# Moving the last block's channel LayerNorm into the first phase, and reordering the loads of the second phase, in a hybrid conformer/RWKV-7 block

## The chip, the core and the metric

The kernel runs on one core of a Trainium2 chip. The metric is the device time of one execution in microseconds (us). Engines are named as in the profile: PE multiplies matrices (PEld loads its weights), DVE is the vector engine, ACT the scalar engine, POOL is GpSimd, and SP issues the DMAs. Before the change the median of 3 runs is 2893.17 us (2893.12 to 2894.62).

## What is computed

One decoder block on x of 2048 tokens by 1024 channels. Cut to what matters here:

```python
h = _rmsnorm(x, norm_g) * (1.0 + scale) + shift
p = h @ w_in                                    # c_val, c_gate, c_og, ts, r_og, g_conv, g_rwkv
u = c_val * sigmoid(c_gate)
u = causal_depthwise_conv(u, conv_k, conv_b)    # width 31
u = _layernorm(u, ln_g, ln_b)                   # over the 1024 channels
u = silu(u) * silu(c_og)
y_conv = u @ w_conv_out
y_rwkv = _rwkv7_branch(...)                     # token shift, delta-rule state, group norm
m = sigmoid(g_conv) * y_conv + sigmoid(g_rwkv) * y_rwkv
x = x + gate * (m @ w_out)
return _rmsnorm(x, final_g)
```

## The kernel before

**Tiles.** The tokens are cut into four blocks (b = 0 to 3) of 512, and each matrix of 1024 channels by 512 tokens into eight tiles (j = 0 to 7) of 128 x 512 float32, 256 KB each. A product in nearly float32 precision is made of three passes: the weights and the data are split into a high and a low part (`w_hi`, `w_lo`, `h_hi`, `h_lo`), and hi*hi, hi*lo and lo*hi are summed in PSUM. A projection is 24 such matmuls (8 k-steps of 3).

**First phase** (lines 425 to 1487). For each block there are four groups g of the RWKV heads (`slot`, line 1388). A group projects the inputs of two head pairs (`k`, `r`, `vv`) and, between them, "fills": channel tiles of the convolution (`c`, two projections each) and gates (`1` to `4`). `FILL` and `LAST` (lines 46 and 47) give the order of the fills. Each conv tile is followed by 31 taps on DVE (`taps`, line 1170), whose result `yj` is stored to DRAM as `y_d[b][j]`. The chain of a group's delta rule runs between the projections. Side work (`sides`, line 1323) does the next block's RMSNorm, the channel LayerNorm of the block before (`lnorm_first`, line 1189, on POOL, in group 1 of blocks 1 to 3), and the splitting of the weights `ro` and `o` into hi and lo parts ahead of their use (`presplit`, line 305: 1, 0, 1, 2 weight tiles in the groups of blocks 1 and 2, and 4, 2, 2, 0 in those of block 3). `lnorm_first` reads the eight `y_d` tiles three times: for the mean, for the variance, and to write `u_d[b][j]`, the normalised and gated tile. It takes its tiles (`lny`, `lnc`, `lnth`) from a ring of seven buffers, `hx`. At the end of the phase `rows0` (line 1456) projects block 0's RWKV output with `w_rwkv_out` (`ro`, tiles `rth`) and its conv output with `w_conv_out` (`co`), and leaves the merged m in `mr`.

**What sets the order.** In the first phase the program writes its own order: a planner keeps a clock for each engine (`note`, line 85, with the rates of lines 48 to 53), the steps of every task are generators that say when they could go on, and `poll` (line 152) emits a step once the planner's PE clock has come that far. Each engine then executes what was emitted for it strictly in that order, and so does SP with its DMAs. In the second phase the framework's scheduler sets the order; it may move loads and small work ahead of where they are written, also before the end of the first phase.

**Second phase** (lines 1491 to 1680). For each block: `cproj` (not for block 0), then the out products `pout` (line 1618: four column blocks of 256, each 96 matmuls of 128 x 256, with weights `o` loaded as `w_hi`/`w_lo`), `addx` (x added to `pout` on DVE), `finish` (the final RMSNorm, eight DVE operations on `xt`, and stores), and `rproj` of the next block, whose result DVE takes out of PSUM as `mr<-rth,ps_main`. `lsplit` loads the next block's z and u tiles (`zt`) and splits them (`m_hi`, `m_lo`, `o_hi`, `o_lo`, `u_hi`, `u_lo`). Block 3's LayerNorm is not done in the first phase; `lnorm` (line 1566) does it here, on tiles of its own (`y0` to `y7`, `ys`, `qs`, `ct`), with POOL for the sums, and with two matmuls, `pmean` and `pvar`. It is written at b = 2, but the scheduler placed most of it beside block 0's out products.

Of the kernel before, what the change touches and what calls it, by code (L numbers as in the profile page):

```python
# [18 lines left out]
P = 128  # L19
D = 1024  # L20
# [23 lines left out]
WB = 6  # L44
KEPT = ("in",)
FILL = ("c", "1", "3", "4", "2", "c", "1", "3", "4", "2")
LAST = ("c", "1", "c", "3", "4", "2", "1", "3", "4", "2")
# [24 lines left out]
def hybrid_block(ctx: ExitStack, tc: tile.TileContext, x, vecs, convk, w2a2, final_g, ada, w_in, w_co, w_ro, w_o, crow, out,  # L72
# [150 lines left out]
    class Ring:  # L223
# [11 lines left out]
        def give(self, *ts):  # L235
            for t in ts:
                self.free.append(max(ready.get(key(t), 0.0), used.get(key(t), 0.0)))

# [950 lines left out]
    def lnorm_first(b):  # L1189

        def yload(j):
            yj = hx.take("lny")
            nc.sync.dma_start(yj, y_dram[b][j])
            return yj

        yield hx.room(3, 1)
        ys, nxt = yload(0), yload(1)
        for j in range(1, KT):
# [5 lines left out]
            nc.gpsimd.tensor_tensor(out=ys, in0=ys, in1=yj, op=ALU.add)  # L1204
# [8 lines left out]
        for j in range(KT):  # L1213
# [5 lines left out]
            nc.gpsimd.tensor_tensor(out=yj, in0=yj, in1=mean, op=ALU.subtract)  # L1219
            yield ok(yj)  # L1220
            nc.scalar.activation(yj, yj, AF.Square)
            if j == 0:
                qs = yj
            else:
                yield ok(yj)
                nc.gpsimd.tensor_tensor(out=qs, in0=qs, in1=yj, op=ALU.add)
                hx.give(yj)
# [6 lines left out]
        for _ in rsteps(rl, qs, rt):  # L1234
            yield idle("DVE", 0.3)
        hx.give(qs, rt)
        for j in range(KT):
            yield hx.room(3, 1)
            yj, ct, th = yload(j), hx.take("lnc"), hx.take("lnth")
            nc.sync.dma_start(ct, co_dram[b][j])  # L1240
            yield ok(yj, rl)
            nc.gpsimd.tensor_tensor(out=yj, in0=yj, in1=mean, op=ALU.subtract)
            yield idle("POOL", 0.3)
            nc.gpsimd.tensor_tensor(out=yj, in0=yj, in1=rl, op=ALU.mult)
# [7 lines left out]
            nc.gpsimd.tensor_tensor(out=yj, in0=yj, in1=ct, op=ALU.mult)  # L1252
# [4 lines left out]
        hx.give(mean, rl)  # L1257
# [65 lines left out]
    def sides(b, g):  # L1323
# [6 lines left out]
        if b and g == 1:  # L1330
            yield from lnorm_first(b - 1)
        if b:
            for _ in range((4, 2, 2, 0)[g] if b + 1 == NB else (1, 0, 1, 2)[g]):
                n_ = later.pop(0)
                for half in range(2):
                    yield from presplit(*n_, half)

    reached, normed = [-1], [0]

    def side_work():  # L1340
        for n in range(4 * NB):
            yield when(lambda: reached[0] >= n)
            yield from sides(n // 4, n % 4)

# [13 lines left out]
    def order(b, g):  # L1358
        todo, cj, gj = list(FILL if b + 1 < NB or g < 3 else LAST), [2 * g, 2 * g + 1], {w: [2 * g, 2 * g + 1] for w in "1234"}

        def fill(n):
            for _ in range(n):
                w = todo.pop(0)
                yield w, (cj if w == "c" else gj[w]).pop(0)
# [60 lines left out]
    with tc.manual_schedule():  # L1425
# [21 lines left out]
        side.append(Task(side_work(), 3))  # L1447
# [8 lines left out]
        def rows0(a, name, gate_, nxt):  # L1456
            new, hfs = ([], []), []
            for n in range(KT):
# [25 lines left out]
              enumerate(("M", "ta", "E2", "k", "r", "vv", "y", "sh"))]  # L1484
        h = rows0(h, "ro", gr_dram[0], u_dram[0])
# [21 lines left out]
    def ldt(name, src):  # L1507
        t_ = ob.tile([P, TB], F32, name=name, tag="ld", bufs=6)
# [39 lines left out]
    b2 = ctx.enter_context(tc.tile_pool(name="b2", bufs=2, reuse_waits="tile"))  # L1548
    hl = ctx.enter_context(tc.tile_pool(name="hl", bufs=1, reuse_waits="tile"))
    pa = ctx.enter_context(tc.tile_pool(name="pa2", bufs=1, space=PSUM, reuse_waits="tile"))  # L1550
# [7 lines left out]
    nc.sync.dma_start(fg, final_g.unsqueeze(0).broadcast_to([P, D]))  # L1558
    def t2(name):
        return b2.tile([P, TB], F32, name=name, tag="t2", bufs=3)  # L1560

# [3 lines left out]

    def lnorm(b):

        y = []
        ys = b2.tile([P, TB], F32, name="ys", tag="ys", bufs=1)
        for j in range(KT):  # L1570
            yj = b2.tile([P, TB], F32, name=f"y{j}", tag=f"y{j}", bufs=1)
            nc.sync.dma_start(yj, y_dram[b][j])
            y.append(yj)
            if j:
# [140 lines left out]
```

## Time and profile before

| what | us |
|---|---|
| median of 3 runs | 2893.17 |
| the profiled execution's own time | 2892.82 |
| its span, from the first to the last instruction | 2890.7 |
| PE busy (94% of the span) | 2725.4 |
| DVE busy (71%) | 2058.8 |
| POOL busy (44%) | 1257.7 |
| ACT busy (38%) | 1090.7 |

The span is 2.1 us shorter than the execution's time. In the profile nearly every row of phase 1 and 2 has line L129, the helper that records each instruction, so instructions are told apart by tile names (out<-in), not by lines. A row of a table by windows gives the busy time of each engine within a stretch, the number of its instructions in brackets, then the granted PE clock (1.00 is full), the share of the 16 DMA engines that was busy, and GB/s. A row of a timeline gives the start and the duration, the engine, the instruction, and in brackets how long the engine had been idle before it and what ended that.

### The profile page before, as it was taken

The page shows a single profiled execution, that of the slowest core. Times are in us where ns is not written, and L with a number is a line of the kernel's source. Part 1 is how long each engine was busy: PE and PEld are TensorE (multiplying, and loading weights), DVE is VectorE, ACT ScalarE, POOL GpSimd, SP SyncE. Part 2 cuts the span into 40 slices and gives each one's busy share as a digit, 9 for nine tenths or more (in the row PEclk, how much of TensorE's full clock was granted, in tenths as well). Part 3 has the DMA queues.
Part 4 walks back from the last instruction along what each step waited for, and adds up shares of the span by engine and source line. Part 5 has one row for each costly group of instructions (what it writes and reads, how often), then busy time and mean ns, then how long its engine had stood idle before and what let it go on. Part 6 is the DMA issues. An engine that isn't in the chain of part 4 may idle for free.

```text
span 2890.7 us, 52304 instructions
## 1 busy us (share of the span) xinstructions
PE 2725.4 (94%) x19472; PEld 2201.6 (76%) x19472; DVE 2058.8 (71%) x3575; ACT 1090.7 (38%) x2180; POOL 1257.7 (44%) x1772
## 2 busy tenths in 40 slices
PE   6999999889999999999999999999999998899998
PEld 5777777667777777787777777777777777698988
DVE  6877787869677878885868787669787666543343
ACT  5545344434243434443434443333434233221211
POOL 0564746533528355444656462648373633100000
PEclk9999999989999999999999999999999999999999
DMA  8786767666757566776756686866666848676665
GB/s 329 255 295 219 281 221 263 237 227 234 231 187 257 183 218 237 250 258 221 252 181 233 205 294 201 273 211 215 205 246 213 294 158 314 234 240 229 215 226 175
DMA packets 361742, 680.47 MB, mean 235 GB/s; under 512 B 134160, under 2 KB 152912, under 8 KB 361488
## 3 DMA queue, kind: packets, MB, share of 16 engines
q1 hardware_dynamic: 361488, 677.13, 69.0%
q8 instruction: 154, 2.52, 0.4%
q14 instruction: 100, 0.82, 0.1%
HBM read 494.34 MB, written 181.54 MB: 234 GB/s over the span
## 4 chain that ended last, share of the span: by engine, by line
PE 32%; DVE 9%; POOL 7%; DMA 5%; issue 3%; ACT 1%; SPq 1%; DVEq 0%; POOLq 0%; ACTq 0%
PE ps_main L129 21%; PE pout L129 5%; DVE acc L129 3%; PE xo L129 2%; PE aux L129 2%; POOL TT L129 2%; POOL itmp L129 1%; PE late L129 1%; SPq L129 1%; DVE S L129 1%; DMA w_lo<-kl_in 1%; POOL oc L129 1%; DVE gst L129 1%; DVE rs_t L129 1%; POOL lny L129 1%
## 5 line engine op out<-in xcount | busy, mean ns | idle before, releaser
L129 PE MATMUL ps_main<-h_hi,w_hi 128*128 128x512 f32 x2432 | 1016.7, 418 | 17.4 <-DVE lora L129 4.6
L129 PE MATMUL ps_main<-h_hi,w_lo 128*128 128x512 f32 x2432 | 967.7, 398 | 20.3 <-POOL w_lo L129 13.6
L129 PE MATMUL ps_main<-h_lo,w_hi 128*128 128x512 f32 x2432 | 963.8, 396 | 2.0 <-DVE h_lo L129 2.0
L129 DVE SCALAR_TENSOR_TENSOR acc<-u,ck,acc 128x512 f32<-128x512 f32 x928 | 697.5, 752 | 25.3
L129 PEld LDWEIGHTS ps_main<-h_hi,w_lo 128*128 128x128 f32 x2432 | 463.4, 191 | 130.7 <-POOL w_lo L129 16.8
L129 PEld LDWEIGHTS ps_main<-h_hi,w_hi 128*128 128x128 f32 x2432 | 464.0, 191 | 128.9 <-issue 10.0
L129 PEld LDWEIGHTS ps_main<-h_lo,w_hi 128*128 128x128 f32 x2432 | 464.9, 191 | 99.8 <-issue 7.8
L129 POOL TENSOR_TENSOR w_lo<-w_st,w_hi 128x1024 fp32r<-128x1024 f32 (+1 forms) x83 | 165.2, 1990 | 302.9 <-ACT w_hi L129 248.7
L129 POOL TENSOR_TENSOR TT<-TT,itmp 128x126 f32<-128x126 f32 (+22 forms) x496 | 207.3, 418 | 38.9
L129 ACT ACTIVATE th<-ps_main 128x512 f32<-128x512 f32 x160 | 95.6, 598 | 333.9 <-PE ps_main L129 281.7
L129 ACT CAST w_hi<-w_st 128x1024 fp32r<-128x1024 f32 (+1 forms) x135 | 127.2, 943 | 243.2 <-DMA w_st<-w_co_t 137.3
L129 POOL TENSOR_TENSOR itmp<-La,TT 128x126 f32<-128x126 f32 (+22 forms) x496 | 200.8, 405 | 37.1 <-issue 6.4
L129 DVE SCALAR_TENSOR_TENSOR S<-xo,pe,Se 64x64 f32<-64x64 f32 x512 | 145.0, 283 | 90.1 <-PE xo L129 65.3
L129 ACT COPY uv<-xo 64x256 f32<-64x256 f32 (+1 forms) x192 | 81.0, 438 | 238.3 <-PE xo L129 164.7
L129 POOL TENSOR_TENSOR lny<-lny 128x512 f32<-128x512 f32 x90 | 119.9, 1340 | 108.9 <-DMA lny<-y_d 87.0
L129 DVE TENSOR_TENSOR w_lo<-w_st,w_hi 128x1024 fp32r<-128x1024 f32 x52 | 72.4, 1392 | 68.3 <-PE ps_main L129 46.5
L129 ACT ACTIVATE Se<-S,pe 128x128 f32<-128x128 f32 x256 | 88.7, 396 | 83.2 <-DVE S L129 82.7
L129 DVE TENSOR_TENSOR As<-aux,maskA 128x512 f32<-128x512 f32 x128 | 82.3, 685 | 52.5 <-PE aux L129 52.5
L129 POOL TENSOR_TENSOR wlo<-wf,wl 64x128 fp32r<-64x128 f32 x64 | 31.2, 488 | 149.6 <-ACT wl L129 147.0
L129 ACT ACTIVATE t<-ps_main,mu 128x512 f32<-128x512 f32 x96 | 65.9, 687 | 77.6 <-PE ps_main L129 68.0
L129 DVE TENSOR_TENSOR xt<-pout,xt 128x256 f32<-128x256 f32 x64 | 24.4, 419 | 99.3 <-PE pout L129 93.2
L129 PEld LDWEIGHTS xo<-S,KR 128*128 128x128 f32 x512 | 76.8, 189 | 23.9 <-DVE S L129 5.3
(298 smaller groups left out, 5029.0 us busy)
## 6 DMA issues: line engine op xcount, KB each, us to landing
w_hi<-kh_in SPq DMA_DIRECT2D x219, 512.0 KB
w_lo<-kl_in SPq DMA_DIRECT2D x219, 512.0 KB
w_st<-w_in_t SPq DMA_DIRECT2D x73, 512.0 KB
kh_in<-w_hi SPq DMA_DIRECT2D x71, 512.0 KB
kl_in<-w_lo SPq DMA_DIRECT2D x71, 512.0 KB
lny<-y_d SPq DMA_DIRECT2D x72, 256.0 KB
w_hi<-kh_ro SPq DMA_DIRECT2D x32, 512.0 KB
w_lo<-kl_ro SPq DMA_DIRECT2D x32, 512.0 KB
```

The costliest lines, as they stand in the source:

```text
L129: r = f(*a, **k)
```

## The change

Five parts.

1. `lnorm` is deleted. `lnorm_first(3, more)` does block 3's LayerNorm as a task of its own (`last_norm`) in the first phase, once all 32 conv tiles are done, on DVE instead of POOL. Its buffers (`more`) are the tiles of the taps' tags `u` and `yj`, three of the `hx` ring lent after block 3's group 0 (`lend`), and three more after the last head pair. For its loads the planner adds `SLACK` to the time at which it takes them to have landed.
2. Block 3's eight conv tiles stand in groups 0, 1 and 2 (three, three and two) instead of two in each group, the LayerNorm of block 2 in its group 0 instead of 1, and all 16 presplits in blocks 1 and 2 (1, 1, 3, 3 in the groups of each).
3. In every `lnorm_first`, the second pass stores y minus mean back to `y_d`, the square goes to a tile of its own (`lnq`), and the third pass no longer subtracts the mean.
4. In the second phase x is loaded ahead of z, `final_g` only after them, and the next block's u is written behind the out products.
5. The ring `ld`, through which z and u tiles come in, has 8 buffers instead of 6.

```diff
+LDB = 8
+SLACK = 2.0
-LAST = ("c", "1", "c", "3", "4", "2", "1", "3", "4", "2")
+LAST = ("c0 10 20 c1 21 11 22 c2 23", "c3 12 24 c4 25 13 26 c5 27", "c6 14 30 c7 31 15 32 33 34 35",
...
-    def lnorm_first(b):
+    def lnorm_first(b, hx):
...
             nc.sync.dma_start(yj, y_dram[b][j])
+            if b + 1 == NB:
+                ready[key(yj)] += SLACK
...
+        eng = nc.vector if b + 1 == NB else nc.gpsimd
...
-            nc.gpsimd.tensor_tensor(out=yj, in0=yj, in1=mean, op=ALU.subtract)
-            yield ok(yj)
-            nc.scalar.activation(yj, yj, AF.Square)
+            eng.tensor_tensor(out=yj, in0=yj, in1=mean, op=ALU.subtract)
+            yield both(ok(yj), hx.room(1))
+            yq = hx.take("lnq")
+            nc.scalar.activation(yq, yj, AF.Square)
+            nc.sync.dma_start(y_dram[b][j], yj)
...
             yield ok(yj, rl)
-            nc.gpsimd.tensor_tensor(out=yj, in0=yj, in1=mean, op=ALU.subtract)
-            yield idle("POOL", 0.3)
-            nc.gpsimd.tensor_tensor(out=yj, in0=yj, in1=rl, op=ALU.mult)
+            eng.tensor_tensor(out=yj, in0=yj, in1=rl, op=ALU.mult)
...
-        if b and g == 1:
-            yield from lnorm_first(b - 1)
+        if b and g == (0 if b + 1 == NB else 1):
+            yield from lnorm_first(b - 1, hx)
+            if b + 1 == NB:
+                yield from lend(3)
         if b:
-            for _ in range((4, 2, 2, 0)[g] if b + 1 == NB else (1, 0, 1, 2)[g]):
+            for _ in range(0 if b + 1 == NB else (1, 1, 3, 3)[g]):
...
+    more = Slots([slot_of(e2, "u", 3)] * 3 + [slot_of(e2, "yj", 1)])
...
+    def last_norm():
+        yield when(lambda: len(convs) == KT * NB and convs[-1].done)
+        yield from lnorm_first(NB - 1, more)
...
-        t_ = ob.tile([P, TB], F32, name=name, tag="ld", bufs=6)
+        t_ = ob.tile([P, TB], F32, name=name, tag="ld", bufs=LDB)
...
-        if b + 1 < NB:
-            ohl = lsplit(z_dram[b + 1], okt(b + 1))
-            uhl = lsplit(u_dram[b + 1], utiles()) if b + 2 < NB else lnorm(b + 1)
         xts = []
...
+        if b + 1 < NB:
+            ohl = lsplit(z_dram[b + 1], okt(b + 1))
+        if b == 0:
+            nc.sync.dma_start(fg, final_g.unsqueeze(0).broadcast_to([P, D]))
...
         if b + 1 < NB:
+            uhl = lsplit(u_dram[b + 1], utiles())
             rall = tail_rs(0, NTT)
```

**SP, start of the out products of block 0.** The loads that stand ahead of the x tiles (`xt_...`) before; `y_...` and `ct` are the old LayerNorm's tiles, `zt` the z tiles of block 1.

```order
L129 DMA zt<-z_d_4_79 128x512
L129 DMA zt<-z_d_5_80 128x512
L129 DMA rth<-gr_d_0_267 128x512
L129 DMA rth<-gr_d_1_268 128x512
L129 DMA y_27755<-y_d_6_193 128x512
L129 DMA y_27758<-y_d_7_194 128x512
L129 DMA ct<-co_d_0_219 128x512
L129 DMA ct<-co_d_1_220 128x512
L129 DMA xt_25415<-x_in 128x512
```

The same place now, from the last store of the new LayerNorm (`u_d_7`) to the first x tile; `rth<-gc_d_7` is the gate of the last `co` projection, `kh_o`/`kl_o` the weights of the first column blocks.

```order
L132 DMA w_hi<-kh_o_0_13678 128x1024
L132 DMA z_d_7_98<-oc 128x512
L132 DMA w_lo<-kl_o_0_13679 128x1024
L132 DMA u_d_7_322<-lny 128x512
L132 DMA rth<-gc_d_7_234 128x512
L132 DMA w_hi<-kh_o_1_17041 128x1024
L132 DMA w_lo<-kl_o_1_17042 128x1024
L132 DMA w_hi<-kh_o_0_17406 128x1024
L132 DMA zt<-z_d_0_75 128x512
L132 DMA zt<-z_d_1_76 128x512
L132 DMA zt<-z_d_2_77 128x512
L132 DMA xt_25534<-x_in 128x512
```

The x loads stand behind three z tiles instead of six z tiles, eight y tiles and two ct tiles. The gate `rth<-gc_d_7` now stands behind two stores. A little further on SP, now, behind the eight x tiles and the z tiles:

```order
L132 DMA zt<-z_d_7_82 128x512
L132 DMA fg<-final_g 128x1024
L132 DMA w_lo<-kl_o_0_17407 128x1024
L132 DMA zt<-u_d_0_299 128x512
L132 DMA zt<-u_d_1_300 128x512
L132 DMA w_hi<-kh_o_1_17880 128x1024
```

`w_lo<-kl_o_0_17407` is the low half of the weights of the second column block; before, both halves of them stood ahead of all z and x tiles.

**DVE, end of block 0's out products**, before: the last four `finish` operations and what follows (`y_...<-th` and `y_...,ct` are the old LayerNorm's, `mr<-rth,ps_main` empties PSUM for PE).

```order
L129 SCALAR_TENSOR_TENSOR xt_25427<-xt_25427,rs_25907,fg 128x512
L129 SCALAR_TENSOR_TENSOR xt_25429<-xt_25429,rs_25907,fg 128x512
L129 SCALAR_TENSOR_TENSOR y_27746<-th,y_27746 128x512
L129 SCALAR_TENSOR_TENSOR y_27749<-th,y_27749 128x512
L129 SCALAR_TENSOR_TENSOR y_27752<-th,y_27752 128x512
L129 TENSOR_TENSOR y_27743<-y_27743,ct 128x512
L129 SCALAR_TENSOR_TENSOR mr_25935<-rth,ps_main 128x512
```

And now:

```order
L132 SCALAR_TENSOR_TENSOR xt_25542<-xt_25542,rs_26109,fg 128x512
L132 SCALAR_TENSOR_TENSOR xt_25544<-xt_25544,rs_26109,fg 128x512
L132 SCALAR_TENSOR_TENSOR xt_25546<-xt_25546,rs_26109,fg 128x512
L132 SCALAR_TENSOR_TENSOR xt_25548<-xt_25548,rs_26109,fg 128x512
L132 SCALAR_TENSOR_TENSOR mr_26137<-rth,ps_main 128x512
```

No LayerNorm operation stands any more between the end of the products and `mr`.

**DVE, during the `co` projections of `rows0`**, before (`S` and `uv` are the chain of the last group, `rth` and `mr` empty PSUM):

```order
L129 SCALAR_TENSOR_TENSOR rth<-rth,ps_main 128x512
L129 SCALAR_TENSOR_TENSOR mr_0_24204<-rth,mr_0_24204 128x512
L129 SCALAR_TENSOR_TENSOR S_405<-xo,pe,Se 64x64 x4
L129 TENSOR_TENSOR uv<-xo,uv 64x256
L129 SCALAR_TENSOR_TENSOR S_405<-xo,pe,Se 64x64 x4
```

And now, where the new LayerNorm's third pass (`lny`) stands between them:

```order
L132 SCALAR_TENSOR_TENSOR S_405<-xo,pe,Se 64x64 x4
L132 SCALAR_TENSOR_TENSOR lny<-lnth,lny 128x512
L132 TENSOR_TENSOR uv<-xo,uv 64x256
L132 TENSOR_TENSOR lny<-lny,lnc 128x512
L132 SCALAR_TENSOR_TENSOR S_405<-xo,pe,Se 64x64 x4
L132 TENSOR_TENSOR lny<-lny,lnr 128x512
L132 TENSOR_REDUCE gst<-uv 128x16
L132 TENSOR_SCALAR gst<-gst 128x16
L132 SCALAR_TENSOR_TENSOR rth<-rth,ps_main 128x512
```

`lny<-lny,lnr` is the first operation on a freshly loaded tile; the emptying of PSUM stands behind it.

112 lines of the change are left out of this document (57 added, 55 removed).

## The prediction

> **What bounds the kernel now.** The page says that PE is busy for 94% of the span, so the first question is where the other 6% lie. I read the table by windows, cut at the stages: the three later blocks of the first phase, `rows0`, and then block 0's out products with the two `rproj` projections that follow them, beside the same stretch of blocks 1 and 2.
>
> ```profile
> 600.50:1158.20 557.70, 537.91 (x4093) 427.50 (x4093) 436.34 (x789) 219.46 (x456) 257.60 (x398) 0.99 0.66 221
> 1158.20:1719.10 560.90, 541.31 (x4094) 430.11 (x4094) 435.92 (x773) 229.96 (x474) 292.85 (x445) 0.98 0.69 233
> 1719.10:2279.20 560.10, 537.69 (x4061) 425.41 (x4060) 418.21 (x709) 210.71 (x421) 308.97 (x450) 0.99 0.69 231
> 2279.20:2397.30 118.10, 111.67 (x858) 87.68 (x857) 73.67 (x122) 32.19 (x60) 42.51 (x47) 0.97 0.64 206
> 2398.20:2486.70 88.50, 62.58 (x434) 57.40 (x434) 69.03 (x99) 39.66 (x86) 36.58 (x24) 0.90 0.86 313
> 2566.00:2624.60 58.60, 57.25 (x432) 54.78 (x432) 25.91 (x57) 17.61 (x49) 0.00 (x0) 1.00 0.74 254
> 2701.40:2757.60 56.20, 56.15 (x433) 53.91 (x431) 20.88 (x49) 12.97 (x41) 0.00 (x0) 1.00 0.60 208
> ```
>
> The columns after the length are PE, PEld, DVE, ACT and POOL. In the first phase PE is idle for some 20 us of each block. Block 0's out products are the odd stage: for the same PE work (434 matmuls beside 432 and 433) they take 88.5 us, the others 58.6 and 56.2. That is some 30 us, the largest loss in one place, and the old LayerNorm runs in it. The waits of PE by releaser, in this stretch, say what it waits for:
>
> ```profile
> PE ps_main L129 <- DVE mr L129: 12.8, 1, 12.8
> PE pmean L129 <- POOL ys L129: 6.3, 1, 6.3
> PE pout L129 <- DVE o_lo L129: 2.6, 3, 1.1
> PE pout L129 <- DVE xt L129: 2.5, 1, 2.5
> PE pout L129 <- DMA w_lo<-kl_o: 1.8, 1, 1.8
> PE pout L129 <- DVE rth L129: 0.5, 1, 0.5
> ```
>
> The two long ones, 12.8 and 6.3 us, are the LayerNorm's: `pmean` stands in PE's queue and waits for POOL's sum, and `mr` stands on DVE behind the old LayerNorm's `y` operations and the `finish` operations. Together with the rest they make 26.5 us.
>
> **Part by part: the first out products.** With `pmean` and the y operations gone, what is late next? Three things.
>
> First, the low halves `o_lo` at the start, which wait for the last `co` projection and its gate. Their 2.6 + 0.5 us I keep. They could shrink, since the same operation takes
>
> ```profile
> L129 DVE TENSOR_TENSOR o_lo<-mr,o_hi 128x512 fp32r<-128x512 f32 x8 | 9.3, 1226 | 0.0
> L129 DVE TENSOR_TENSOR o_lo<-mr,o_hi 128x512 fp32r<-128x512 f32 x8 | 5.5, 692 | 4.9 <-ACT o_hi L129 4.9
> ```
>
> 1226 ns in this stretch, where POOL works, and 692 ns in block 2's, where POOL rests. They could also grow: `rth<-gc_d_7` now stands behind two stores that wait for POOL and DVE, and `o_lo` stands behind its consumer. I take 3.1 us, between 0.6 and 6.
>
> Second, the loads. The weights of the second column block need buffers that the last `co` projection holds, so they cannot be fetched before about 2397.
>
> ```profile
> 2400.00:2420.00 20.00, 11.95 (x92) 10.87 (x91) 12.47 (x14) 5.45 (x11) 13.08 (x9) 0.94 1.03 386
> 2420.00:2440.00 20.00, 15.75 (x106) 14.58 (x105) 16.66 (x21) 11.13 (x29) 10.65 (x7) 0.84 0.95 355
> 2400.26 0.32 SPq L129 DMA_DIRECT2D w_hi<-kh_o  x1
> 2413.57 5.02 SPq L129 DMA_DIRECT2D xt<-x_in  x8
> ```
>
> The DMA engines are full there (1.03 and 0.95 of them, 386 and 355 GB/s). From `w_hi` of the second column block to its `w_lo`, SP now issues 0.5 MB, three z, eight x and five z tiles of 0.25 MB, `fg` of 0.5 MB and `w_lo` of 0.5 MB: 5.5 MB, which at 386 GB/s take 15 us, so `w_lo` lands at about 2414. The first column block's 96 matmuls take a quarter of a column's
>
> ```profile
> 2566.00:2624.60 58.60, 46.05 (x384) 45.84 (x383) 6.04 (x16) 1.00 0.74 254
> ```
>
> 46.05 us (this row counts `pout` alone), 11.5 us, and end with the 3.1 us of waits at 2398.2 + 14.6 = 2412.8. That is a wait of about 2 us, and I add 1.5 for the later column blocks, whose weights stand behind u and z tiles: 3.5 us, between 0 and 8. The whole stage bears this out: 88.5 us at 313 GB/s moved 27.7 MB; without eight y tiles and the four ct tiles that came before its end (3.1 MB) 24.6 MB are left, 64 us at 386 and 69 at 355 GB/s.
>
> Third, the end. After the products DVE does 12 operations on four columns, eight `finish` operations and `mr`, as in block 1, whose 58.6 us hold such a wait already. I leave it there.
>
> Then the clock. After a short wait the matmuls come slower for a while:
>
> ```profile
> 2265.61 0.47 PE L129 MATMUL ps_main<-h_hi,w_hi 128*128 128x512 f32 x1 [1.74 <-DMA w_hi<-kh_in]
> 2266.96 0.51 PE L129 MATMUL ps_main<-h_hi,w_lo 128*128 128x512 f32 x1 [0.65 <-DMA w_lo<-kl_in]
> 2267.66 0.63 PE L129 MATMUL ps_main<-h_lo,w_hi 128*128 128x512 f32 x1
> ```
>
> 0.63 us instead of the usual 0.39, after two waits of 1.74 and 0.65 us; the stage as a whole was granted 0.90. I price one such stretch at 1.6 us (0 to 4). The Trainium skill, "TensorE: Matmul & The Clock Gate", section "What's actually happening", has the clock halved only after an idle window of about 3.4 us. By that rule waits of 2 and 1.5 us would cost nothing more than themselves, and the sum would be 1.6 us lower. The rows show the slow matmuls after less, and the measurement decides.
>
> So the stage takes 58.6 + 3.1 + 3.5 + 1.6 = 66.8 us instead of 88.5: **21.7 us gained**, between 11.9 (76.6 us) and 29.3 (59.2 us).
>
> **The projections behind it.**
>
> ```profile
> 2486.74 79.24 PE ps_main L129 x336
> 2624.60 76.82 PE ps_main L129 x336
> ```
>
> The chain of waits gives 79.24 us for those after block 0 and 76.82 after block 1; with no wait of 12.8 us ahead of them they should run alike: **2.4 us gained** (0 to 2.8).
>
> **What the first phase gets.** PE gets the mean and variance matmuls, 592 ns each: 1.2 us. DVE gets 57 operations (15 on sums and means, 7 on squares, 24 in the third pass, 11 for the square root): at 692 ns 39 us, and if all met POOL, at 1226 ns 70 us. The time for them:
>
> ```profile
> L129 PE MATMUL late<-lny,ones x12: 592/592/697, 874.4 to 1981.3; 128*128 128x512 f32 x12
> 2190.00:2397.30 207.30, 197.95 (x1411) 156.55 (x1410) 145.17 (x251) 64.55 (x129) 86.17 (x108) 0.98 0.68 224
> 2297.75 1.68 SPq L129 DMA_DIRECT2D y_d<-yj x1
> L129 DVE SCALAR_TENSOR_TENSOR acc<-u,ck,acc 128x512 f32<-128x512 f32 x928 | 697.5, 752 | 25.3
> ```
>
> Between 2190 and 2397 DVE is idle for 62 us, and in this stretch it still does taps until the last `yj` is stored at 2297.75. In the new order the last tap stands 15 projections earlier, near 2197, and some 1.6 tiles of 31 taps at 752 ns, 37 us, leave the stretch. So 39 to 70 us meet 99 us of idle time. I take 2 us for PSUM emptied late (0 to 8).
>
> Those 37 us of taps go to the three groups ahead, and there DVE rises from 314 to 351 of 420 us:
>
> ```profile
> 1719.10:1861.00 141.90, 134.48 (x1016) 106.44 (x1015) 111.71 (x189) 53.88 (x110) 62.95 (x84) 0.99 0.72 234
> 1861.00:2000.00 139.00, 134.62 (x1014) 106.28 (x1013) 92.04 (x157) 50.29 (x104) 91.83 (x135) 0.99 0.67 225
> 2000.00:2139.60 139.60, 134.81 (x1020) 106.92 (x1019) 110.19 (x188) 55.68 (x106) 77.89 (x114) 0.99 0.67 227
> 840.00:900.00 60.00, 58.80 (x283) 46.84 (x283) 57.30 (x86) 21.16 (x42) 48.70 (x70) 1.00 0.85 292
> ```
>
> 84%. The last row is the densest stretch of block 1: DVE at 57.3 of 60 us, and PE still at 58.8. I take 1 us (0 to 6). The presplits, the earlier LayerNorms, their 24 new stores and the 24 subtractions that POOL loses I cost at nothing: PE's work covers them, and blocks with 4, 4 and 8 presplits took 557.7, 560.9 and 560.1 us, no more than 3.2 us apart. If that cover fails, 5 us; at best 3 us are gained in block 3.
>
> **The sum**, against the profiled execution's own 2892.82 us: -21.7 - 2.4 + 1.2 + 2 + 1 = -19.9, so 2872.9. The median of the runs is 0.35 us above that execution, so the forecast is 2873. All good ends give -33.9 (2859), all bad ones +8.3 (2901).
>
> **The rivals.** *The loads set the pace.* If the first products run at the 313 GB/s that the stage had on the whole, 24.6 MB take 78.6 us, 9.9 are gained, and the time is 2885. For it: the DMA engines are full. Against: 313 is a mean over pauses. Chance 0.12.
>
> *No new wait.* The stage is as short as block 1's, 59 us, and the phase ahead costs nothing but its matmuls: -29.5 - 2.4 + 1.2, 2862. For it: z and u tiles of later blocks need not come in this stage, so the bytes can be fewer. Chance 0.2.
>
> *The LayerNorm stalls DVE in the first phase* (the slower one). A tile that lands late now holds DVE, with the chain and the emptying of PSUM behind it.
>
> ```profile
>   DMA lny<-y_d: 87.0, 24
> ```
>
> POOL sat idle 24 times for such a tile, 87.0 us, 3.6 us a time. If each of 23 waits held DVE as long, 83 us with the dear 70 us of work would need 153 of the 99 us: 54 us over, and 2893 - 24 + 1 + 54 = 2924. It decides for slower from 2.3 us a wait at 70 us of work, or from 3.7 at 39 us. Against it: the third pass now loads a tile ahead, SLACK puts the step 2 us later, and 3.6 - 2 = 1.6 us a wait fit in. The Trainium skill, "SBUF — State Buffer", section "SBUF: two separate sides", makes a two-input DVE operation and a POOL operation exclude each other for a whole instruction. The 1226 beside 692 ns agree; by that rule the dear end is the likelier one, and it keeps this rival's chance at 0.12 where I would have said 0.08.
>
> *Nothing is left*: the first phase loses some 20 us in many small waits. Three blocks within 3.2 us of each other speak against it. Chance 0.08.
>
> **How the numbers follow.** The forecast (2867 to 2881) has 0.48. Faster by over 0.2% (5.8 us, about what a measurement here can tell from no change) are the forecast, the first two rivals: 0.48 + 0.12 + 0.2 = 0.80. Within 0.2%: 0.08. Slower: 0.12. The range 2857 to 2890 takes in the forecast, the first two rivals with their spread and part of the fourth, and leaves out the slow one.
>
> **What would show it.** Right: no LayerNorm tile in the second phase, block 0's stage at 62 to 72 us, `mr` no longer a wait of PE, and the longest wait there by `w_lo` or `xt`; the 336 matmuls behind it at 77 us; block 3 within 3 us of 560, and `rows0` near 120. Wrong: DVE idle for long before `lny`, ended by a DMA, with PE waiting for `rth` or `mr` in `rows0`; or a stage of 78 us and more with `w_lo` as its releaser.

## The result, and the profile after

| | before | after |
|---|---|---|
| median of 20 runs (us) | 2893.31 | 2888.58 |
| lowest to highest | 2884.17 to 2899.40 | 2878.86 to 2901.92 |
| the profiled execution | 2892.82 | 2893.26 |
| its span | 2890.7 | 2891.5 |

The ratio is 0.9986, with a 95% interval of 0.9975 to 0.9998: 4 us faster, less than the 0.2% that the prediction called no change. The time lies within the range given, but the gain is a fifth to a quarter of the forecast. The profiled execution of after lies 4.7 us above its median, so its stages are a little long.

The same table by windows as in the prediction, for after: three blocks of the first phase, `rows0`, block 0's out products with two `rproj` projections, and the 336 matmuls behind them (columns: length; busy time of PE, PEld, DVE, ACT, POOL; granted clock, DMA share, GB/s).

```profile
602.40:1166.00 563.60, 540.33 (x4090) 427.37 (x4089) 438.74 (x792) 225.74 (x468) 262.23 (x407) 0.99 0.70 234
1166.00:1730.40 564.40, 541.47 (x4097) 427.81 (x4096) 441.20 (x771) 229.65 (x474) 291.45 (x434) 0.99 0.71 239
1730.40:2299.90 569.50, 539.56 (x4059) 425.51 (x4058) 438.69 (x743) 210.65 (x422) 285.60 (x441) 0.99 0.68 228
2299.90:2420.80 120.90, 110.31 (x863) 87.30 (x862) 91.92 (x148) 43.93 (x75) 36.80 (x34) 0.99 0.74 252
2420.80:2489.20 68.40, 57.83 (x433) 54.41 (x433) 34.45 (x72) 25.28 (x63) 0.00 (x0) 0.95 0.95 348
2489.20:2565.60 76.40, 76.40 (x338) 63.27 (x338) 28.29 (x36) 12.78 (x15) 0.00 (x0) 1.00 0.66 221
```

The second phase did nearly what was forecast. The fifth row is the stage that took 88.5 us: 68.4 now, with POOL idle (0.00), and the sixth is the chain's 79.24 us, 76.4 now. PE's waits in the stage of 68.4 us:

```profile
PE pout L132 <- DVE xt L132: 6.2, 3, 3.5
PE ps_main L132 <- DVE mr L132: 2.8, 1, 2.8
PE pout L132 <- DMA w_lo<-kl_o: 0.9, 1, 0.9
PE pout L132 <- ACT o_hi L132: 0.7, 1, 0.7
PE pout L132 <- DVE o_lo L132: 0.7, 1, 0.7
```

`pmean` and the wait of 12.8 us for `mr` are gone; 2.8 us for `mr` are left, where the prediction's sign was none. What is late next is the loads, as the chain of waits says (start, duration):

```profile
2420.74 5.32 DMA zt<-z_d
2426.07 6.92 DMA xt<-x_in
2433.05 7.24 DMA w_lo<-kl_o
2440.33 12.34 PE pout L132 x94
```

They act through DVE and ACT. PE waits 6.2 us for `xt` (x added to the product), and `xt` stands on DVE behind the split of a z tile, `m_lo`. Two rows of DVE's timeline and one of ACT's:

```profile
2435.00 0.69 DVE L132 TENSOR_TENSOR m_lo<-zt,m_hi 128x512 fp32r<-128x512 f32 x1 [6.82 <-ACT m_hi L132]
2435.61 0.75 DVE L132 TENSOR_TENSOR xt<-pout,xt 128x256 f32<-128x256 f32 x2
2434.35 1.93 ACT L132 CAST m_hi<-zt 128x512 fp32r<-128x512 f32 x3 [6.97 <-DMA zt<-z_d]
```

The change moved the x loads ahead of the last five z loads, but on DVE the splits of these z tiles stand ahead of the additions of x and between them. So the additions wait for z all the same.

The first phase gave it back. Its blocks 1 to 3 are 5.9, 3.5 and 9.4 us longer than before and `rows0` 2.8 us. Block 0, where the two programs have the same instructions in the same order, is 1.9 us longer (602.4 instead of 600.5), which is the scatter of one execution. The first out product starts at 2420.8 instead of 2397.3: 23.5 us late. If the 4.7 us by which this execution lies above the median are all in the first phase, that is some 19 us in the median (an estimate). From there on after gains 22.7.

### The profile page after: what moved, and what is told of

It is laid out like the page before. It is cut to its first block, busy times and chain, and to the rows that moved or that the text cites. A ratio compares the mean times of both kernels' runs of the same rounds, so it can differ in the third digit from the quotient of the medians.

```text
span 2891.5 us, 52406 instructions
## 1 busy us (share of the span) xinstructions
PE 2722.4 (94%) x19472; PEld 2195.2 (76%) x19472; DVE 2067.5 (72%) x3598; ACT 1092.9 (38%) x2181; POOL 1195.6 (41%) x1725
## 5 line engine op out<-in xcount | busy, mean ns | idle before, releaser
L132 PE MATMUL ps_main<-h_hi,w_hi 128*128 128x512 f32 x2432 | 1016.3, 418 | 16.7 <-DVE lora L132 4.6
L132 PEld LDWEIGHTS aux<-KR,BK 64*128 64x128 f32 x1024 | 66.3, 191 | 44.3 <-POOL KR L132 21.1
L132 PE MATMUL aux<-KR,BK 64*128 64x128 f32 x1024 | 80.0, 290 | 20.7 <-POOL KR L132 14.0
```

The lines of the kernel that those rows point to most:

```text
L132: r = f(*a, **k)
```

## The experiments

Differences are of medians, to the kernel before in the same rounds; the ratio (with its 95% interval) is that of the runs. The last two columns are read from the one profiled execution of each run: when PE starts the first out product, and how long the program takes from there to its end. A profiled execution can lie some us from its kernel's median, 12 us at most (f_presplit_back).

| run | against before (us) | ratio | first out product at | from there |
|---|---|---|---|---|
| before | | | 2397.3 | 493.4 |
| after | -4.7 | 0.9986 (0.9975 to 0.9998) | 2420.8 | 470.7 |
| a_phase2_only | -15.6 | 0.9938 (0.9916 to 0.9960) | 2398.2 | 473.5 |
| b_form | -14.9 | 0.9948 (0.9935 to 0.9961) | 2389.2 | 480.0 |
| c_presplit | -5.8 | 0.9981 (0.9966 to 0.9996) | 2398.5 | 483.0 |
| d_conv | -27.0 | 0.9898 (0.9873 to 0.9923) | 2386.0 | 470.0 |
| e_no_last_norm | -12.8 | 0.9949 (0.9931 to 0.9968) | 2395.7 | 470.5 |
| f_presplit_back | +6.8 | 1.0019 (1.0006 to 1.0033) | 2410.9 | 471.1 |
| g_old_passes | +21.4 | 1.0078 (1.0062 to 1.0093) | 2440.3 | 468.0 |
| h_ln_pool | +9.0 | 1.0030 (1.0020 to 1.0040) | 2414.5 | 478.5 |
| i_both_back | +5.6 | 1.0015 (1.0003 to 1.0028) | 2398.5 | 488.8 |
| j_after_redealt | +29.8 | 1.0098 (1.0084 to 1.0113) | 2438.7 | 474.7 |
| k_phase2_redealt | +32.7 | 1.0111 (1.0096 to 1.0125) | 2439.2 | 486.7 |
| l_conv_redealt | +16.7 | 1.0051 (1.0037 to 1.0065) | 2416.3 | 491.5 |
| r_after_334 | +42.3 | 1.0141 (1.0123 to 1.0160) | 2471.8 | 462.8 |
| s_conv_alone | -0.6 | 0.9996 (0.9983 to 1.0008) | 2411.7 | 483.6 |
| n_norm_planned | -19.6 | 0.9938 (0.9924 to 0.9952) | 2396.1 | 473.5 |
| o_stores_planned | -9.2 | 0.9976 (0.9962 to 0.9990) | 2417.3 | 471.9 |
| t_norm_no_dve | -8.7 | 0.9979 (0.9962 to 0.9996) | 2404.4 | 475.1 |
| m_slack0 | +7.2 | 1.0028 (1.0011 to 1.0044) | 2428.7 | 473.8 |

The first theory was: the first phase loses time in the parts that were costed at nothing (the moved presplits, the new passes), and the LayerNorm itself is cheap. The rival: the LayerNorm costs.

### First four: the parts without the LayerNorm

**a_phase2_only.** The first phase of before; of block 3's LayerNorm nothing:

```diff
-        side.extend((Task(side_work(), 3), Task(last_norm(), 3)))
+        side.append(Task(side_work(), 3))
...
-            uhl = lsplit(u_dram[b + 1], utiles())
+            uhl = lsplit(u_dram[b + 1] if b + 2 < NB else y_dram[b + 1], utiles())
```

> First phase as in the kernel before, second phase as in the kernel after (x first, u behind the products, 8 load buffers). Block 3's LayerNorm is left out altogether: its conv tiles are read unnormalised and ungated. Theory (the gain of the second phase came in full, and the changed first phase gave it back): the first phase is the one of before, `pout` starts near 2397, and the second phase is shorter by the 23.8 us that the trace of after shows from the first out product to the end of the second projections: 2893.3 - 23.8 = 2869.5, between 2866 and 2873. Rival (the longer first phase of the one profiled execution of after is chance, and the second phase gained less than that profile shows): 2880 or more.

Measured: 15.6 us gained by the medians, 18 by the ratio, at most 24 by its interval. That lies between the theory's range (20 to 27 gained) and the rival's (13 or less). Its profile has the first out product at 2398.2 (as before) and the phase behind it 19.9 us shorter. So the second phase does gain most of what after's profile shows, and the loss in after is in the first phase.

**c_presplit**, the same and the presplits moved:

```diff
-            for _ in range((4, 2, 2, 0)[g] if b + 1 == NB else (1, 0, 1, 2)[g]):
+            for _ in range(0 if b + 1 == NB else (1, 1, 3, 3)[g]):
```

> As a_phase2_only (block 3's LayerNorm left out), with one part of the change to the first phase: all 16 presplits of weights in blocks 1 and 2 (1, 1, 3, 3 in the groups of each) and none in block 3. Theory (the moved presplits are what lengthens blocks 1 and 2): blocks 1 and 2 longer by the 5.9 and 3.5 us that the trace of after shows, block 3 shorter by 3 at most, so the time is that of a_phase2_only + 6 to 9 us. Rival (the density of block 3 alone costs): within 3 us of a_phase2_only.

10 us above a_phase2_only, just over what the theory had, and yet the theory falls: the first out product starts at 2398.5, 0.3 us from a_phase2_only's. The loss is behind it, where PE waits in the out products for

```profile
PE pout L131 <- DVE xt L131: 13.1, 2, 12.3
```

12.3 us at once. SP had been held until 2407.05 by the store of the last `oc`, and the z and x tiles behind it came late. A number that fits, with the wrong place: only the stages told it.

**d_conv**, a_phase2_only with `LAST`, `order` and block 2's LayerNorm as in after:

> As a_phase2_only (block 3's LayerNorm left out), with one part of the change to the first phase: block 3's conv tiles in groups 0 to 2 (3, 3, 2) and block 2's LayerNorm in its group 0. Theory (DVE, made denser in block 3's first three groups, holds the delta-rule chain up): block 3 longer by 5 to 9 us, the time that of a_phase2_only + 5 to 9 us. Rival (the order of the conv tiles is free, presplits and stores cost): within 3 us of a_phase2_only.

Neither: 11 us below a_phase2_only. In the profile its block 3 took 547.4 us, where a_phase2_only's took 559.5.

**e_no_last_norm**, after with the two lines of a_phase2_only and without `lend(3)`:

> The kernel after without block 3's LayerNorm (left out altogether: its conv tiles are read unnormalised and ungated); every other part of the change is in it. Theory (the LayerNorm itself is cheap, as the prediction had it, 3 us, and the parts around it cost): after - 3 us, near 2885. Rival (the LayerNorm on DVE at the end of block 3 and beside the first projections behind it is what costs): after - 9 to 12 us, near 2878.

8 us below after by the medians, 11 by the ratios, at the rival's end. The LayerNorm isn't cheap, though the parts around it seem to cost as well (14 us between d_conv and this).

### Next four: whole kernels with one part taken back

f_presplit_back, with the row of c_presplit undone and `lend(2)`:

> The kernel after, whole in its computation, with the presplits of weights where the kernel before had them (1, 0, 1, 2 in the groups of blocks 1 and 2, and 4, 2, 2, 0 in block 3), for which the LayerNorm is lent two buffers of the ring instead of three. After stood 4.7 us below before; c_presplit stood 9.8 us above a_phase2_only. Theory (the moved presplits cost 10 us here too): 14 to 15 us below before, near 2878 where before is 2893. Rival (in c_presplit the 9.8 us were lost in the second phase, beside a late store, and have nothing to do with blocks 1 and 2): within 3 us of after, 2 to 8 us below before.

g_old_passes; for blocks 0 to 2:

```diff
-            yield both(ok(yj), hx.room(1))
-            yq = hx.take("lnq")
-            nc.scalar.activation(yq, yj, AF.Square)
-            nc.sync.dma_start(y_dram[b][j], yj)
-            hx.give(yj)
+            yield ok(yj)
+            yq = yj
+            nc.scalar.activation(yj, yj, AF.Square)
...
+                nc.gpsimd.tensor_tensor(out=yj, in0=yj, in1=mean, op=ALU.subtract)
```

> The kernel after, whole in its computation, with the LayerNorms of blocks 0 to 2 in the old form of passes (the square in place, no stores of y minus mean, and the mean subtracted again in the third pass); block 3's keeps the new form. Between d_conv and e_no_last_norm lie the presplits and the new form, 14.3 us, of which c_presplit gives 9.8 to the presplits. Theory (the 24 stores, 6.3 MB, and the dearer wait for a free buffer cost the rest): 4 us below after, 8 to 10 us below before. Rival (the form is free, as predicted, and the rest is interaction or scatter): within 3 us of after; or it gains nothing and the subtractions that return to POOL cost 1 to 3 us.

h_ln_pool, with `eng = nc.gpsimd`:

> The kernel after, whole in its computation, with block 3's LayerNorm on POOL instead of DVE. e_no_last_norm showed that this LayerNorm costs 8 us in the first phase. Theory (it costs because its waits for loads and its operations hold up DVE, and the chain and the emptying of PSUM behind them): on POOL 4 to 8 us below after. Rival (it costs by its loads and by the buffers, or POOL's slower operations make the end of the first phase later): no gain, 0 to 10 us above after.

> f_presplit_back and g_old_passes together: of the change there are left the second phase, block 3's conv tiles in groups 0 to 2, block 2's LayerNorm in group 0, and block 3's LayerNorm on DVE. Theory (the parts add): d_conv, 27.0 us below before, plus the LayerNorm's own 8 us: 19 us below before. Rival (the LayerNorm's cost comes from block 3 being full, and with eight presplits back in block 3 it costs more): 10 us below before or less.

All four are slower than after, by 10 to 26 us, against every theory; the rivals of h_ln_pool and i_both_back had the direction. In g_old_passes a place can be named: block 3's LayerNorm stored its last tile at 2441.7, and the phase ended with

```profile
PE pout L132 <- ACT o_hi L132: 23.6, 1, 23.6
```

PE idle for 23.6 us, since the first phase ends only when every task has. In after the last tile was stored at 2415.3, 5.5 us ahead of the first out product: the LayerNorm runs to the very end of the phase. The other three must be read by stages, as c_presplit was. i_both_back reaches the first out product 22 us earlier than after and loses 18 us behind it (488.8 instead of 470.7), h_ln_pool 6 us earlier and loses 8 (478.5). The profiled execution of f_presplit_back is faster than that of after (2883.75 against 2893.26), so it can't show the loss. The parts don't add up, which brought the question whether leaving out a part is a fair test at all: every edit makes the planner deal the whole first phase anew from its place on.

### The order dealt anew, with nothing added or taken away

```diff
-DMA_RATE = 330e3
+DMA_RATE = 326e3
```

in after (j_after_redealt), a_phase2_only (k_phase2_redealt) and d_conv (l_conv_redealt). b_form keeps 330; it adds only the new passes to a_phase2_only.

> The kernel after, whole in its computation and with every part of the change, but with the planner's figure for the DMA rate 1.2% lower (326 instead of 330). No instruction is added or taken away; only the order in which the planner emits the first phase is dealt anew. After stood 4.7 us below before. Theory (the changed first phase loses a few us in many small waits whose sum hangs on how the order happens to fall): its time differs from after's by 5 us or more, in either direction, with the same second phase. Rival (the loss has a definite place, the LayerNorm at the end of the phase or the moved presplits, which this edit leaves alone): within 3 us of after, 2 to 8 us below before.

> a_phase2_only (the first phase of before, the second of after, block 3's LayerNorm left out) with the planner's DMA rate 1.2% lower. a_phase2_only stood 15.6 us below before. Theory (scatter of the dealing): differs from it by 5 us or more. Rival (differences of 10 us between these kernels have causes in their parts): 12 to 19 us below before.

> d_conv (as a_phase2_only, with block 3's conv tiles in groups 0 to 2 and block 2's LayerNorm in group 0; block 3's LayerNorm left out) with the planner's DMA rate 1.2% lower. d_conv stood 27.0 us below before. Theory (its gain of 11 us over a_phase2_only was a lucky dealing): 12 to 22 us below before. Rival (the earlier conv tiles free the end of block 3 and do gain): 24 to 30 us below before.

> a_phase2_only (block 3's LayerNorm left out) with the LayerNorms of blocks 0 to 2 in the new form of passes (y minus mean stored, the square in a tile of its own, no subtraction in the third pass). Theory (the form is free beside other work, as predicted): within 3 us of a_phase2_only, 12 to 19 us below before. Rival (its 24 stores and the third buffer that it holds cost): 4 us or more above a_phase2_only. If the redealt kernels scatter by 5 us or more, neither is shown by this run alone.

And later the same constant at 334e3:

> The kernel after, whole in its computation, with the planner's DMA rate 1.2% higher (334 instead of 330). At 326 it stood 29.8 us above before. Theory (each dealing is a draw, and 330 is a value for which it fell well): 10 to 40 us above after, as at 326. Rival (the time falls steadily with the rate assumed): 10 us or more below after.

The planner's figure moved by 1.2% costs 34, 48 and 44 us at 326, and 47 at 334. Both sides of 330 lose, so that the time doesn't follow the rate assumed; 330 is a value at which the deal fell well. l_conv_redealt is outside both of its ranges: it loses 30 us before the first out product and 22 behind it, so a deal also moves the second phase. j_after_redealt's stretch of block 0 and its blocks 1 and 3:

```profile
0.00:607.00 607.00, 541.69 (x3680) 427.47 (x3681) 476.30 (x790) 279.48 (x515) 325.19 (x417) 0.97 0.75 260
607.00:1175.20 568.20, 540.49 (x4089) 428.63 (x4089) 433.91 (x793) 225.20 (x467) 259.98 (x404) 0.98 0.70 230
1740.30:2323.30 583.00, 541.29 (x4066) 428.11 (x4066) 459.48 (x766) 216.67 (x430) 287.92 (x438) 0.97 0.70 231
```

PE's work is nearly the same (541.69 us in block 0 where after has 543.81, 541.29 in block 3 where after has 539.56); the blocks take longer, block 3 583.0 us where after's took 569.5. It isn't many small waits, as the theory had it: one wait stands out in block 3 (19.1 us, the longer of the two in the first row), one in block 1 (8.2, second row), and in r_after_334 one at the end of the first phase (29.3, third row), as in g_old_passes.

```profile
PE late L132 <- POOL uv L132: 19.7, 2, 19.1
PE late L132 <- DVE Tn L132: 10.5, 4, 8.2
PE pout L132 <- ACT o_hi L132: 29.3, 1, 29.3
```

In r_after_334 block 3's LayerNorm stored its last tile at 2465.8, 6 us ahead of the first out product: there, too, PE waits for the end of this LayerNorm. So differences of 10 us between the eight runs above can be the deal's as well as the part's. So can b_form's 0.7, in which a first phase 9 us shorter than a_phase2_only's and a second phase 6.5 us longer cancel. This takes the ground from the readings of c_presplit, d_conv and e_no_last_norm, and from f to i but for the wait in g.

### The same order, with single parts not issued

The planner's lanes got a twin that notes an instruction and doesn't issue it, so that its clocks run as before:

```diff
-                r = f(*a, **k)
+                r = None if self.plan_only else f(*a, **k)
```

In n_norm_planned all of `lnorm_first(3)` goes through it, in o_stores_planned the 24 stores, in t_norm_no_dve the 57 DVE operations. In the traces every other instruction of DVE, ACT and POOL in the first phase stands in after's order, and so does every other DMA but one load of a gate at its very end.

> The kernel after with block 3's LayerNorm planned as before, and its instructions (57 on DVE, 25 on ACT, 2 on PE, 48 DMAs) not issued: every other instruction of the first phase stands in the same order as in after. Block 3's conv tiles are read unnormalised and ungated. Theory (the LayerNorm's own operations and waits cost, DVE held up at the end of block 3 and in rows0): 6 to 12 us below after, 11 to 17 us below before, with the gain in block 3 and rows0. Rival (the order costs, not the operations): within 3 us of after, 2 to 8 us below before.

> The kernel after with the 57 DVE operations of block 3's LayerNorm planned and not issued; its loads, stores, ACT operations and matmuls are issued, and every other instruction stands in after's order. (Left out so are its sums, the subtraction of the mean, the division and the gate.) n_norm_planned, without the whole LayerNorm, stood 14 to 15 us below after. Theory (DVE's operations hold the chain and the emptying of PSUM up): 11 to 15 us below after, near n_norm_planned. Rival (its 48 DMAs, 12.6 MB, and ACT cost as much): 4 to 8 us below after. Second rival (DMA and buffers alone): within 3 us of after.

The LayerNorm costs 15 us by the medians (-19.6 against -4.7), more than the theory of n_norm_planned said, and 14 by the ratios (0.9938 against 0.9986); the two intervals put it between some 9 and 19. The profiles agree if the stretch is cut where the LayerNorm begins, at its first load, right behind the store of the last conv tile (`y_d<-yj`). Block 3 up to there, and from there to the first out product, in after:

```profile
1730.40:2214.40 484.00, 457.08 (x3527) 360.49 (x3529) 388.56 (x645) 175.85 (x349) 247.54 (x382) 0.99 0.67 223
2214.40:2420.80 206.40, 192.79 (x1398) 152.33 (x1398) 142.06 (x245) 78.73 (x148) 74.86 (x93) 0.99 0.73 254
```

in t_norm_no_dve

```profile
1727.80:2205.80 478.00, 456.67 (x3531) 360.46 (x3533) 388.43 (x645) 175.81 (x349) 246.63 (x382) 0.99 0.68 225
2205.80:2404.40 198.60, 191.52 (x1399) 153.94 (x1397) 94.42 (x188) 78.20 (x148) 67.71 (x93) 0.98 0.78 266
```

and in n_norm_planned:

```profile
1732.30:2205.50 473.20, 452.47 (x3534) 357.26 (x3535) 387.11 (x644) 175.61 (x349) 245.49 (x378) 1.00 0.68 226
2205.50:2396.10 190.60, 186.58 (x1395) 151.14 (x1391) 93.27 (x188) 61.63 (x123) 67.57 (x93) 1.00 0.63 211
```

The first rows hold the same instructions in the same order, and still lie 484.0, 478.0 and 473.2 us long: that is the scatter of single executions. The second rows are the LayerNorm's: 206.4 us with all of it, 198.6 without DVE's operations, 190.6 without any, so 15.8 us in all. 8.0 us of it are its 48 DMAs, 25 ACT operations and two matmuls; the medians (-8.7 against -19.6) give 10.9 and the ratios 12. DVE's operations make 7.8 us in the profiles, 4 in the medians and 2 in the ratios, whose intervals overlap; how much of it is real stays open. So t_norm_no_dve lies between the ranges of its two rivals, and far from its theory: the loads, stores and ACT operations cost at least as much as DVE's work. (That they cost the same with DVE's operations between them as without is assumed.)

How the DMAs and ACT cost PE time shows in `rows0`. PE's waits there, in t_norm_no_dve

```profile
PE ps_main L132 <- ACT h_hi L132: 3.2, 1, 3.2
PE xo L132 <- DVE uv L132: 1.4, 1, 1.4
PE pout L132 <- ACT o_hi L132: 0.7, 1, 0.7
```

and in n_norm_planned:

```profile
PE pout L132 <- ACT o_hi L132: 0.7, 1, 0.7
PE ps_main L132 <- ACT h_hi L132: 0.4, 1, 0.4
PE ps_main L132 <- DVE h_lo L132: 0.3, 1, 0.3
```

2.8 us more in one wait for `h_hi`; after has this wait too, with 2.8 us. Whom ACT waited for there says its timeline (start, duration; in brackets how long ACT had been idle and for what), in t_norm_no_dve

```profile
2294.00 2.62 ACT L132 CAST h_hi<-hf 128x512 fp32r<-128x512 f32 x4 [6.86 <-DMA hf<-z_d]
```

and in n_norm_planned:

```profile
2290.81 1.98 ACT L132 CAST h_hi<-hf 128x512 fp32r<-128x512 f32 x3 [4.56 <-DMA hf<-z_d]
2293.12 0.62 ACT L132 CAST h_hi<-hf 128x512 fp32r<-128x512 f32 x1 [0.33 <-DMA hf<-z_d]
```

It waited for `rows0`'s own data, which land later beside the LayerNorm's DMAs (an idle time of 6.86 us instead of 4.56): from 2270 to 2300 the DMA engines moved 11.40 MB in t_norm_no_dve and 9.26 MB in n_norm_planned.

The rest of the 8.0 us is PE's own busy time, 191.52 against 186.58. 1.2 us of that are the two matmuls themselves (592 ns each). The 654 matmuls of the projections (`ps_main`) took 165.67 against 161.68 us, 4.0 more. Most of that (half of 6.8 us) lies in one stretch at a granted clock of 0.50, which begins with the end of that wait. One row of PE's timeline and one by windows:

```profile
2294.67 0.80 PE L132 MATMUL ps_main<-h_hi,w_hi 128*128 128x512 f32 x1 [3.20 <-ACT h_hi L132]
2294.10:2300.90 6.80, 6.23 (x16) 4.72 (x17) 2.69 (x4) 4.16 (x7) 0.00 (x0) 0.50 0.90 267
```

In this stretch of n_norm_planned the clock was 1.00 throughout. So the late loads cost PE some 3 us of waiting and about as much again in slow matmuls. That the wait halved the clock is inferred from its place (see also the last section). All this is read from one pair of executions; over all of them the mean granted clock was 0.984 in t_norm_no_dve (12 executions) and 0.986 in n_norm_planned (6).

> The kernel after with the 24 new stores of y minus mean (blocks 0 to 2) planned and not issued, every other instruction in the same order. The third pass of these LayerNorms so reads y with the mean still in it. Theory (6.3 MB more traffic on queues that are full to 0.7 costs in blocks 1 to 3): 3 to 6 us below after. Rival (hidden, as predicted, and b_form's 15.5 us below before against a_phase2_only's 15.6 says so): within 2 us of after.

4.4 us below after by the medians, 3 by the ratios, with overlapping intervals: the stores cost between nothing and some 8 us, and this is not settled. (For the 15.5 us of b_form in this expectation, the table has 14.9.)

> The kernel after, whole in its computation, with SLACK = 0: the planner puts each step of block 3's LayerNorm where it takes its load to have landed, not 2 us later. The order of everything ahead of it is unchanged. In after DVE waited three times for its tiles, 11.6 us. Theory (the waits for loads cost little, its DVE operations cost): within 3 us of after. Rival (without slack DVE waits at many of its 23 loads): 5 us or more above after.

```diff
-SLACK = 2.0
+SLACK = 0.0
```

12 us above after, as the rival said. It isn't many waits, though. DVE's waits for the tiles, in m_slack0 and in after:

```profile
DVE lny L132 <- DMA lny<-y_d: 12.2, 3, 8.3
```

```profile
DVE lny L132 <- DMA lny<-y_d: 11.6, 3, 5.5
```

The sums are nearly equal, but one wait of 8.3 us fell where it hurt. `rows0` took 129.9 us with PE at a clock of 0.93, and PE's longest wait there is by DVE's `lny`:

```profile
2298.80:2428.70 129.90, 115.77 (x861) 90.31 (x859) 82.95 (x137) 43.36 (x74) 38.12 (x37) 0.93 0.68 228
PE ps_main L132 <- DVE lny L132: 4.2, 1, 4.2
```

While DVE stood idle for that tile, `mr<-rth,ps_main` behind it couldn't empty PSUM for PE. That is the mechanism of the prediction's slower rival, once. DVE's order differs from after's from the LayerNorm's first operations on (the last 200 us of the phase), so the rest of the 12 us may be the deal's, and the slack's own worth is not shown.

> The kernel before, whole in its computation, with one part of the change: block 3's conv tiles in groups 0 to 2 (3, 3, 2) and block 2's LayerNorm in its group 0. Its first phase has the instructions of d_conv in d_conv's order; block 3's LayerNorm stays in the second phase. d_conv stood 11.4 us below a_phase2_only. Theory (the gain is the first phase's and holds): 11 us below before, which is 6 us below after. Rival (the second phase takes it back, since its LayerNorm then meets the loads): within 3 us of before.

The rival: no change. By its profile block 3 took 553.2 us, 6.9 less than before, and `rows0` 131.9, 13.8 more; the same first phase in d_conv took 547.4 and 119.5. What `rows0` lost has a place, the old LayerNorm's `pmean`, for which PE now waits at the end of `rows0`:

```profile
PE pmean L130 <- POOL ys L130: 20.7, 1, 20.7
```

Whether the earlier tiles gain without it is not shown. No whole kernel that was tried beats after.

## Why the prediction failed, step by step

**The stage of the first out products.** Forecast 66.8 us, measured 68.4; 21.7 to be gained, 20.1 gained. The low halves took 1.4 us of waits instead of 3.1 (`o_lo` takes 686 ns now, with POOL idle, where it took 1226), and the loads 7.1 (`xt` and `w_lo`) instead of 3.5. The prediction's sum had the loads at `w_lo`; the longest wait is `xt`, behind the z tiles on DVE. The term for slow matmuls, 1.6 us, was right in kind. Behind the wait of 3.5 us the clock was halved:

```profile
2436.50:2443.30 6.80, 3.96 (x16) 3.37 (x17) 4.27 (x8) 3.88 (x12) 0.00 (x0) 0.50 1.03 397
```

Its sixteen matmuls took 3.96 us; at the 0.12 us that one takes on the mean of this stage they would take 1.9, so this cost some 2 us (an estimate). PE's work in the whole stage is only 0.6 us above block 1's (57.83 against 57.25). The Trainium skill's rule ("TensorE: Matmul & The Clock Gate", "What's actually happening": the clock is halved after an idle window of about 3.4 us) fits the trace in this place. It doesn't fit it elsewhere, where the clock was halved after waits of 1.8 to 3.2 us (last section).

**The projections behind it.** 2.4 us forecast, 2.8 measured. Together the second phase was to gain 24.1. It gained 22.7 in after's profile, and 18.3 to 21.5 in those of a_phase2_only, n_norm_planned, o_stores_planned, t_norm_no_dve and m_slack0.

**The LayerNorm in the first phase.** This step failed. "39 to 70 us meet 99 us of idle time. I take 2 us": it priced DVE's work against DVE's idle time, and that work did come out as bounded, 142.06 - 93.27 = 48.8 us. That is 856 ns an operation, between the 692 and 1226 ns of the prediction. But idle time of the engine isn't what sets the price. In the same order its instructions cost 14 to 15 us, where 3.2 stood (2 for DVE and 1.2 for the matmuls). The 48 DMAs (12.6 MB) and 25 ACT operations of the moved step had no term at all; with the two matmuls they make 8 us of it in the profiles and 11 to 12 in the runs. The way from them to PE is the late load of `rows0`, the wait for it and the halved clock behind it. Without its instructions nothing else is lost: in n_norm_planned's profile the first out product starts at 2396.1, where before has 2397.3, and the 19.9 us gained behind it are its whole gain.

**The parts at nothing.** That presplits, new passes and earlier conv tiles cost nothing on the whole is not contradicted: after without the LayerNorm's instructions (0.9938) stands where the first phase of before with the new second phase stands (0.9938), with some 7 us of uncertainty. But the two have different deals, and those alone differ by more. Of each part alone nothing is shown.

**The rivals.** What happened is nearest to the one called *Nothing is left*, which had 0.08: the first phase lost some 20 us. It said many small waits; most of the loss is the LayerNorm's 15 us. That the time still lies within the stated range is no merit of the sum, which was 15 us off. I argued against this rival that three blocks with different presplits lay within 3.2 us of each other. That was evidence of one deal, not of the next. The slower rival (DVE held by late tiles) didn't occur in after: DVE waited three times, 11.6 us, instead of 23 times. In the new second phase *No new wait* was too good by 9 us, and *The loads set the pace* too bad: the stage ran at 348 GB/s, not 313. Of the signs, block 3 "within 3 us of 560" was wrong (569.5); `rows0` near 120 and the 336 matmuls at 77 us were right (120.9 and 76.4).

## What to carry to other kernels

Work moved into a stage where PE is busy to 96% and all engines run in a fixed order is not free because an engine is idle there for long enough: price its DMAs as well, and the loads that they delay, and count a wait of PE of some 3 us about twice, for the slow matmuls behind it. Where a planner deals the order, an edit changes the deal, and its scatter (here 30 to 50 us for a constant moved by 1%) can exceed the effect; to price a part, keep the order and don't issue the part. Read a difference in the stage where it arises: c_presplit had the expected total in the wrong phase. And before a profile's difference is put down to a part, compare the stretch ahead of the part's first instruction: there it is scatter.

## What was not expected of the hardware

The granted clock was halved after waits of PE of 1.8 to 3.2 us. In block 3 and `rows0` there are four such stretches in t_norm_no_dve (three here, and the one behind the wait for `h_hi` above) and one in n_norm_planned (last row):

```profile
1761.60:1768.40 6.80, 6.60 (x75) 5.60 (x76) 6.14 (x12) 1.76 (x3) 0.93 (x2) 0.50 0.72 258
2065.40:2068.80 3.40, 3.40 (x10) 2.64 (x9) 3.07 (x7) 0.00 (x0) 0.52 (x1) 0.50 0.97 352
2161.00:2164.40 3.40, 3.40 (x9) 2.63 (x8) 2.47 (x4) 2.17 (x5) 2.98 (x8) 0.50 0.17 70
1765.70:1769.10 3.40, 3.40 (x10) 2.66 (x9) 3.29 (x7) 1.63 (x3) 0.19 (x1) 0.51 0.43 133
```

Each begins within 2 us of the end of a wait of PE: of 3.12, 1.98 and 3.11 us in the first three rows, of 1.82 in the last, and of 3.20 for `h_hi`. Only the one for `h_hi` has to do with block 3's LayerNorm; the others lie ahead of its first load. Not every such wait is followed by one: behind after's wait of 2.8 us for `mr` the clock was 1.00 for all of the 76.4 us. What decides it is not shown. The scatter of executions goes with it: in the twenty of after, the mean granted clock was 0.981 in the longest (2901.92 us) and 0.988 in one of the shortest (2879.19).
